# Attention: score steps of 128 and 256 columns run as one of 384, and the rotary step reads its product from PSUM

## The chip, the cores and the metric

The kernel runs on one core of a Trainium2 chip, as one program and one launch. The metric is the device time of that program in microseconds (us), as the median of several runs. Its engines are TensorE (PE; its weight loads are shown apart as PEld), VectorE (DVE), ScalarE (ACT), GpSimd (POOL) and the DMA queues, of which SP's issues most loads. Each engine takes its instructions in the order in which the program lists them; that order is made when the program is built.

## The reference

Two layers of width 1024 over 512 positions. Layer 0 is attention, layer 1 a gated delta rule; each is followed by a SwiGLU network. The change touches layer 0 alone, which has two kinds of heads, eight of each, 64 wide:

```python
def attention_head_groups(h, positions, w_in, w_out):
    proj = h @ w_in                                # q, k, v of both kinds
    qa, ka = partial_rope(qa, positions), partial_rope(ka, positions)
    oa = moba_attention(qa, ka, va)                # with 512 positions: causal softmax attention
    ob = stick_breaking_attention(qb, kb, vb)
    return concatenate([oa, ob]) @ w_out

# stick breaking, for the queries of one block, against all keys up to it
z = q @ k.T * scale
log_1m = where(causal, log_sigmoid(-z), 0.0)
log_after = cumsum(log_1m, reverse=True) - log_1m
w = where(causal, exp(log_sigmoid(z) + log_after), 0.0)
out = w @ v

# rope, on the first 16 of a head's 64 rows
[x1 * cos - x2 * sin, x2 * cos + x1 * sin, rest]
```

## The kernel before

All activations lie transposed, features on the 128 partitions and the 512 positions in the columns. Products are made in float32 from halves: a value is split into a rounded high part and the rest (`split`, line 246: ScalarE's copy writes the high part, VectorE's subtraction the low one, line 254), and each product is three matmuls of 512 columns (`gemm`, lines 337 to 340).

Layer 0 first makes q, k and v of the first pair of heads (lines 634 to 643). From then on it works in four pairs (line 809): for each of the two heads of a pair `moba` and `stick`, and then, as work to fill TensorE's waits, the four projections of the next pair (`proj`, line 703). `spread` (line 698) ties the 32 k-steps of these four projections to the 16 score products of the pair's two heads, so two k-steps may start after each of these (`gates`, `behind`). What runs when beyond that is set by the program's scheduler, by its own estimate of durations. Of the last pair, the first blocks of the output projection take that place (line 831). `proj` asks for weights two ahead; these come by DMAs that POOL issues (lines 291 and 293, the second adds in the DMA).

`finish` (line 648) takes a projection's product out of its PSUM bank (tag `mm`, three banks, line 199). For q and k of `moba` (rotary) ScalarE copies it to SBUF (line 651), VectorE swaps rows of the copy (653), POOL multiplies them by the sines (654) while VectorE multiplies the copy by the cosines (655), and VectorE adds the two (656). The result is split for each head.

`moba` (line 743) goes in four steps i, of 128, 256, 384 and 512 score columns: two matmuls and between them one of 128 columns that adds the causal mask in bfloat16 (lines 739 to 741) into the one bank `s`; the row maximum (753), the exponential with its sum (755), a reciprocal, the scaling, transposes into the one bank `pt` (768), and the split into `ph` and `pl`. Then `pv_out` multiplies by v (lines 730 to 732).

`stick` (line 773) goes in four steps j = 3, 2, 1, 0 of 128, 256, 384 and 512 columns, in two banks `z`: scores and mask as above, then on ScalarE absolute value, exponential and logarithm (789 to 791), VectorE's 792, a split into `ssh`, `ssl`, matmuls that add the sums over later keys to the bank (798), an exponential that frees it (800), and a split that POOL makes (804, 805; for the last head ScalarE and VectorE). It ends in `pv_out`. The tensors `sph`, `spl`, `ssh` and `ssl` hold the steps behind each other in the order 3, 2, 1, 0.

Between the heads VectorE also makes the conditioning vectors of both layers, one product of 1024 columns at a time (`ada`, line 210).

Of the kernel before, what the change touches and what calls it, by code (L numbers as in the profile page):

```python
# [71 lines left out]
ADA0 = 4  # L72
NACT = (1, 6)
# [462 lines left out]
def attention(e, x0ctx):  # L536
    nc, tc, V, G, A, PE, I = e.nc, e.tc, e.V, e.G, e.A, e.PE, e.I
    from contextlib import ExitStack
    with ExitStack() as ctx:
        p1 = ctx.enter_context(e.pool("at1"))  # L540

        C = p1.tile([128, T], F32, name="C")
# [49 lines left out]
        first = e.start()  # L592
# [19 lines left out]
        with e.psum_pool("start") as sp:  # L612
# [32 lines left out]
                    e.act_set()  # L645
            fin = ctx2.enter_context(e.pool("afin"))

            def finish(ps, name, scale, rope, dma):
                if rope:
                    q = fin.tile([128, T], F32, name="rq", bufs=2)  # L650
                    A.activation(q, ps, AF.Copy, scale=scale)
                    sw = fin.tile([128, T], F32, name="rs", bufs=1)
                    V.stream_shuffle(sw, q, swap)
                    G.tensor_tensor(sw, sw, S, op=OP.mult)
                    V.tensor_tensor(q, q, C, op=OP.mult)
                    V.tensor_tensor(q, q, sw, op=OP.add)
                    ps, scale = q, 1.0
                rows = [(slice(64 * head, 64 * head + 64), slice(64 - 64 * head, 128 - 64 * head)) for head in range(2)]
                if (name, 0) in twice:
                    assert scale == 1.0  # L660
                    for head, (rs, other) in enumerate(rows):
                        h, l = twice[name, head]
                        e.split(ps[rs], h[rs], l[rs])
                        if dma:
                            nc.sync.dma_start(h[other], h[rs])
                        else:
                            A.activation(h[other], ps[rs], AF.Copy)
                    return [twice[name, head] for head in range(2)]

                both = [qk.tile([128, T], F32R, name=f"{name}{head}", bufs=1) for head in range(2)]  # L670
                for t, (rs, other) in zip(both, rows):
                    A.activation(t[rs], ps[rs], AF.Copy, scale=scale)
                    V.scalar_tensor_tensor(t[other], ps[rs], scale, t[rs].bitcast(F32), op0=OP.mult, op1=OP.subtract)
                return both
# [10 lines left out]
            cur = [finish(pq[i], *KINDS[i], False) for i in range(4)]  # L685
# [10 lines left out]
        steps = []  # L696
# [6 lines left out]
        def proj(pair, i):  # L703
            w = e.load_w(("attn_in", (pair - 1) * 4 + i))
            ps = e.mm_tile()
            e.gemm(ps, w, hs, FULL)
            return finish(ps, *KINDS[i], False)

        def vproj(i):
            ws = [e.load_w(("attn_v", i, j)) for j in (0, 4)]  # L710
# [13 lines left out]
        def pv_out(chunk, r0, tag, ph, pl, at):  # L724

            o = psum.tile([128, T], F32, name="o", tag="o", bufs=1)
            vh, vl = vtile("ab"[chunk // 4], chunk % 4)
            for j in range(4):
                q = slice(j * 128, T)
                PE.matmul(o[:, q], vh[:, j], at(ph, j), start=j == 0, stop=False)  # L730
                PE.matmul(o[:, q], vl[:, j], at(ph, j), start=False, stop=False)
                PE.matmul(o[:, q], vh[:, j], at(pl, j), start=False, stop=j == 3)
            rs = slice(r0, r0 + 64)
            e.split(o[rs], ot[chunk][0][rs], ot[chunk][1][rs])

        def scores(ps, x, xs, y, ys, at, mask):

            xh, xl = x
            PE.matmul(ps, xh[:, xs], y[:, ys], start=True, stop=False)
            PE.matmul(ps[:, at], e.identb, mask, start=False, stop=False)  # L740
            steps[-1].append(PE.matmul(ps, xl[:, xs], y[:, ys], start=False, stop=True).ins)

        def moba(pair, h, q, k):

            ph = work.tile([128, 1664], F32R, name="ph", tag="ph", bufs=1)
            pl = work.tile([128, 1664], F32R, name="pl", tag="pl", bufs=1)
            for i in range(4):
                n = 128 * (i + 1)
                qs = slice(i * 128, n)
                s = psum.tile([128, T], F32, name="s", tag="s", bufs=1)  # L750
                scores(s[:, :n], q[h], qs, k[h], slice(0, n), qs, causal)
                st = work.tile([128, 3], F32, name="st", tag="st", bufs=4)
                V.tensor_reduce(st[:, 0:1], s[:, :n], AX.X, OP.max, negate=True)
                p = work.tile([128, T], F32, name="p", tag="p", bufs=2)
                A.activation(p[:, :n], s[:, :n], AF.Exp, bias=st[:, 0:1], accum_out=st[:, 1:2])
                ins = V.reciprocal(st[:, 2:3], st[:, 1:2])
                step = 4 * (2 * pair + h) + i - ADA0
                if 0 <= step < 24:
                    with tc.issue_after(ins.ins):
                        e.ada(0, 2 + step // 8, step % 8)  # L760
                if NACT[0] <= 2 * pair + h < NACT[1]:
                    A.activation(p[:, :n], p[:, :n], AF.Copy, scale=st[:, 2:3])
                else:
                    V.tensor_scalar(p[:, :n], p[:, :n], st[:, 2:3], None, op0=OP.mult)
                pt = psum.tile([128, T], F32, name="pt", tag="pt", bufs=1)
                for j in range(i + 1):
                    js = slice(j * 128, j * 128 + 128)
                    PE.transpose(pt[:, js], p[:, js], e.ident)
                src = pt[:, :n].rearrange("p (j q) -> p j q", q=128)
                e.split(src, *(x.rearrange("p (j q) -> p j q", q=128)[:, i:4 * i + 1:3] for x in (ph, pl)))  # L770
            pv_out(pair, h * 64, "m", ph, pl, lambda x, j: x[:, 512 * j:512 * j + 512 - 128 * j])

        def stick(pair, h, q, k):
            off = {3: 0, 2: 128, 1: 384, 0: 768}

            def at(x, j):
                return x[:, off[j]:off[j] + T - 128 * j]

            wh = work.tile([128, 1280], F32R, name="sph", tag="sph", bufs=1)
            wl = work.tile([128, 1280], F32R, name="spl", tag="spl", bufs=1)  # L780
            sh = work.tile([128, 1280], F32R, name="ssh", tag="ssh", bufs=1)
            sl = work.tile([128, 1280], F32R, name="ssl", tag="ssl", bufs=1)
            for j in (3, 2, 1, 0):
                n = T - 128 * j
                bank = ("pt", "s", "z", "z")[j] if (pair, h) == (3, 1) else "z"
                z = psum.tile([128, T], F32, name="z", tag=bank, bufs=2 if bank == "z" else 1)
                scores(z[:, :n], k[h], slice(j * 128, j * 128 + 128), q[h], slice(j * 128, T), slice(0, 128), strictT)
# [7 lines left out]
                for jj in range(3, j, -1):  # L795
                    mms = [(z[:, (jj - j) * 128:n], nones, at(x, jj)) for x in (sh, sl)] + mms
                for i, (o, m, x) in enumerate(mms):
                    PE.matmul(o, m, x, start=False, stop=i == len(mms) - 1, skip_group_check=True)
                w = e.wpool.tile([128, T], F32, name="sq", tag="sq", bufs=3)
                A.activation(w[:, :n], z[:, :n], AF.Exp)  # L800
                if (pair, h) >= LATE:
                    e.split(w[:, :n], at(wh, j), at(wl, j))
                else:
                    G.tensor_scalar(at(wh, j), w[:, :n], 1.0, 1.0, op0=OP.mult, op1=OP.mult)
                    G.tensor_tensor(at(wl, j), w[:, :n], at(wh, j).bitcast(F32), op=OP.subtract)
            pv_out(4 + pair, h * 64, "s", wh, wl, at)

        vproj(0)
        for p in range(4):
# [499 lines left out]
```

## Time and profile before

| what | us |
|---|---|
| median of 3 runs (1411.13 to 1413.59) | 1411.75 |
| the profiled execution, its own time | 1410.65 |
| its span, first to last instruction | 1408.8 |
| PE busy in the span | 1360.9 |
| DVE busy | 818.6 |
| ACT busy | 605.4 |
| POOL busy | 292.0 |

The stage that the change touches runs from about 66 us of the span, where the first projections end, to about 282, where the output projection has TensorE to itself. The views used below are the page's first part (busy time by engine), the table of windows (busy time by engine in each stretch, with the TensorE clock that was granted as a share of full speed), the waits (who waited for whom, how long, how often), the timeline (start, duration, what it is; in brackets the idle time before it and what ended that), and the groups of instructions by line and shape (busy time, mean duration in ns of one; then the idle time before them).

### The profile page before, as it was taken

To read this page: it belongs to the slowest core of one execution; us is meant where nothing else is said; L and a number is where in the kernel's file an instruction comes from. 1 tells how busy PE (TensorE), PEld (TensorE's weight loads), DVE (VectorE), ACT (ScalarE), POOL (GpSimd) and SP (SyncE) were. 2 spreads that over 40 slices of the span, in tenths; PEclk is the share of its full clock that TensorE was granted. 3 is DMA by queue.
4 is the path that set the end of the run, shared out by engine and by line. 5 is a ranking of instruction groups with operands and counts; after the bars stand their busy time and mean duration, and the time that the engine had idled before them with its cause. 6 is when DMAs were issued, how large, how long until landed. Compare 5 with 4: busy or idle time off the path is not lost.

```text
span 1408.8 us, 19224 instructions
## 1 busy us (share of the span) xinstructions
PE 1360.9 (97%) x7354; PEld 1158.4 (82%) x7354; DVE 818.6 (58%) x1422; ACT 605.4 (43%) x1162; POOL 292.0 (21%) x279
## 2 busy tenths in 40 slices
PE   7999999899999999999999899999999999999997
PEld 4787787698888888889888787888998888888887
DVE  6777879655667667323878796446783333333233
ACT  5577888744222222223557533356662222222221
POOL 4024444110111111000024735311001111110010
PEclk9999999999999999999999999999999999999999
DMA  9537674042667666434522314312452333333332
GB/s 367 164 75 193 171 181 159 30 166 65 219 217 241 233 236 221 131 106 152 177 62 75 105 60 120 106 46 90 151 180 73 93 94 101 96 99 94 97 102 68
DMA packets 58734, 190.66 MB, mean 135 GB/s; under 512 B 7081, under 2 KB 11305, under 8 KB 58642
## 3 DMA queue, kind: packets, MB, share of 16 engines
q1 hardware_dynamic: 53376, 173.56, 38.0%
q0 software_dynamic: 4112, 14.82, 4.8%
q8 instruction: 58, 0.95, 0.3%
q10 hardware_dynamic: 1154, 1.05, 0.2%
q14 instruction: 34, 0.28, 0.1%
HBM read 184.11 MB, written 5.29 MB: 134 GB/s over the span
## 4 chain that ended last, share of the span: by engine, by line
PE 84%; DVE 6%; ACT 4%; DMA 3%; POOL 1%; issue 1%; SPq 0%; DVEq 0%; ACTq 0%; POOLq 0%
PE mm L337 21%; PE mm L338 21%; PE mm L340 21%; DMA wh<-in_attn_in_dram 1%; PE f L340 1%; PE f L338 1%; PE f L337 1%; PE mm L1117 1%; PE mm L1115 1%; PE mm L1116 1%; PE bank L949 1%; DVE DT L1009 1%; DMA call<-in_consts_dram 1%; PE bank L1051 1%; PE mm L719 1%
## 5 line engine op out<-in xcount | busy, mean ns | idle before, releaser
L249 ACT ACTIVATE wh<-raw 128x1024 fp32r<-128x1024 f32 (+1 forms) x203 | 211.5, 1042 | 535.5 <-PE mm L338 488.9
L254 DVE TENSOR_TENSOR wl<-raw,wh 128x1024 fp32r<-128x1024 f32 (+1 forms) x193 | 231.9, 1202 | 192.1 <-ACT wh L249 176.0
L337 PE MATMUL mm<-hh,wh 128*128 128x512 f32 (+1 forms) x776 | 290.0, 377 | 0.7 <-ACT wh L249 0.6
L338 PE MATMUL mm<-hl,wh 128*128 128x512 f32 (+1 forms) x776 | 288.0, 374 | 0.0
L340 PE MATMUL mm<-hh,wl 128*128 128x512 f32 (+1 forms) x776 | 243.2, 374 | 0.0
L337 PEld LDWEIGHTS mm<-hh,wh 128*128 128x128 f32 x776 | 146.6, 189 | 25.2 <-ACT wh L249 1.1
L338 PEld LDWEIGHTS mm<-hl,wh 128*128 128x128 f32 x776 | 146.9, 189 | 24.2
L340 PEld LDWEIGHTS mm<-hh,wl 128*128 128x128 f32 x776 | 142.7, 189 | 25.2
L214 DVE CUSTOM_DVE_ANT_0 aw<-aw,cond 128x1024 f32<-128x1024 f32 x96 | 126.2, 1333 | 5.9 <-DMA aw<-in_ada_w_dram 5.8
L251 POOL TENSOR_SCALAR ah<-ac 128x512 fp32r<-128x512 f32 x36 | 53.3, 1482 | 363.9 <-DVE ac L497 363.9
L338 PE MATMUL mm<-h1l,wh 128*128 128x512 f32 x320 | 124.5, 389 | 0.0
L337 PE MATMUL mm<-h1h,wh 128*128 128x512 f32 x320 | 124.5, 389 | 0.0
L338 PE MATMUL mm<-al,wh 128*128 128x512 f32 (+1 forms) x354 | 124.0, 355 | 0.0
L337 PE MATMUL mm<-ah,wh 128*128 128x512 f32 (+1 forms) x354 | 123.7, 355 | 0.2 <-ACT ah L249 0.2
L497 DVE TENSOR_TENSOR ac<-sg,mm 128x512 f32<-128x512 f32 x40 | 27.5, 688 | 146.5 <-PE mm L340 143.1
L340 PE MATMUL mm<-h1h,wl 128*128 128x512 f32 x320 | 105.0, 389 | 0.0
L340 PE MATMUL mm<-ah,wl 128*128 128x512 f32 (+1 forms) x354 | 103.8, 355 | 0.0
L337 PEld LDWEIGHTS mm<-ah,wh 128*128 128x128 f32 x354 | 66.5, 188 | 9.9 <-ACT ah L249 0.5
L338 PEld LDWEIGHTS mm<-al,wh 128*128 128x128 f32 x354 | 66.6, 188 | 9.4
L340 PEld LDWEIGHTS mm<-ah,wl 128*128 128x128 f32 x354 | 63.9, 188 | 9.4
L338 PEld LDWEIGHTS mm<-h1l,wh 128*128 128x128 f32 x320 | 60.1, 188 | 12.5
L337 PEld LDWEIGHTS mm<-h1h,wh 128*128 128x128 f32 x320 | 60.0, 188 | 12.5
(395 smaller groups left out, 2484.5 us busy)
## 6 DMA issues: line engine op xcount, KB each, us to landing
aw<-in_ada_w_dram SPq DMA_DIRECT2D x96, 512.0 KB
raw<-in_ffn_in_dram SPq DMA_DIRECT2D x88, 512.0 KB
raw<-in_ffn_out_dram SPq DMA_DIRECT2D x36, 512.0 KB
raw<-in_gdn_in_dram SPq DMA_DIRECT2D x26, 512.0 KB
raw<-in_gdn_z_dram SPq DMA_DIRECT2D x16, 512.0 KB
raw<-in_gdn_out_dram SPq DMA_DIRECT2D x16, 512.0 KB
raw<-in_ffn_out_dram SPq DMA_DIRECT2D x18, 384.0 KB
wh<-in_attn_in_dram POOLq DMA_DIRECT2D x12, 512.0 KB, 4.8
```

The costliest lines, as they stand in the source:

```text
L214: return V.tensor_tensor_reduce(w, w, cond, 1.0, 0.0, OP.mult, OP.add, mod[:, j:j + 1])
L249: ins = A.activation(h, src, AF.Copy)
L251: G.tensor_scalar(h, src, 1.0, 1.0, op0=OP.mult, op1=OP.mult)
L254: (G if eng == "p" else V).tensor_tensor(l, src, h.bitcast(F32), op=OP.subtract)
L337: PE.matmul(ps, wh[k][:, 0], xh[:, cs], start=first and i == 0, stop=False)
L338: PE.matmul(ps, wh[k][:, 0], xl[:, cs], start=False, stop=False)
L340: PE.matmul(ps, wl[j][:, 0], x[j][0][:, cs], start=False, stop=last and j == order[-1])
L497: ins = V.tensor_tensor(ac, sg, pu, op=OP.mult)
L719: PE.matmul(ps, xh[:, t], wl, start=False, stop=False)
L949: PE.matmul(ps[:, c], lhs[:, cs], rhs[:, cs], start=True, stop=True)
L1009: V.tensor_tensor(d, DS[:, :m, m:m + 1].to_broadcast([128, m, w]), DV[:, m:m + 1, m:].to_broadcast([128, m, w]), op=OP.mult)
L1051: PE.matmul(p4[:, c], U[h][lo, c], x[lo, c, lo], start=True, stop=True)
```

## The change

In `finish`, ScalarE's copy is gone. VectorE's row swap and its multiplication by the cosines read the product in PSUM. The factor 0.125 of q, which that copy applied, is applied by the copies and the subtraction that split q; both copies of a head now stand ahead of the subtraction.

In `moba`, steps 1 and 0 share the bank `s` (256 and 128 columns, behind each other). Their maxima, exponentials, reciprocals and scalings stay apart, but the transposes go into one bank `pt` and one split of 384 columns takes them out. In `stick`, steps 3 and 2 share one bank `z`; absolute value, exponentials, logarithm, VectorE's operation and both splits run once over 384 columns, and so do the matmuls with `ntri`. Steps 2 and 3 of `moba` and 1 and 0 of `stick` stay alone.

The mask comes ahead of the scores, as the matmul that starts the bank; for a merged step one matmul of 256 columns writes it for both. `ph` and `pl` are packed to 1280 columns, in an order in which each group's columns lie together, so that `pv_out` reads blocks of 128 columns at a distance of two or four blocks.

```diff
-            def finish(ps, name, scale, rope, dma):
+            def finish(ps, name, scale, rope):
                 if rope:
                     q = fin.tile([128, T], F32, name="rq", bufs=2)
-                    A.activation(q, ps, AF.Copy, scale=scale)
                     sw = fin.tile([128, T], F32, name="rs", bufs=1)
-                    V.stream_shuffle(sw, q, swap)
+                    V.stream_shuffle(sw, ps, swap)
                     G.tensor_tensor(sw, sw, S, op=OP.mult)
-                    V.tensor_tensor(q, q, C, op=OP.mult)
+                    V.tensor_tensor(q, ps, C, op=OP.mult)
                     V.tensor_tensor(q, q, sw, op=OP.add)
-                    ps, scale = q, 1.0
+                    ps = q
...
-                        e.split(ps[rs], h[rs], l[rs])
-                        if dma:
-                            nc.sync.dma_start(h[other], h[rs])
-                        else:
-                            A.activation(h[other], ps[rs], AF.Copy)
+                        for to in (rs, other):
+                            A.activation(h[to], ps[rs], AF.Copy, scale=scale)
+                        V.scalar_tensor_tensor(l[rs], ps[rs], scale, h[rs].bitcast(F32), op0=OP.mult, op1=OP.subtract)
...
+        def masked(ps, first, n, mask):
+            PE.matmul(blocks(ps, first, 1, n), e.identb, mask[:, None, :].to_broadcast([128, n, 128]),
+                      start=True, stop=False, skip_group_check=True)
...
-            PE.matmul(ps, xh[:, xs], y[:, ys], start=True, stop=False)
-            PE.matmul(ps[:, at], e.identb, mask, start=False, stop=False)
-            steps[-1].append(PE.matmul(ps, xl[:, xs], y[:, ys], start=False, stop=True).ins)
+            PE.matmul(ps, xh[:, xs], y[:, ys], start=False, stop=False, skip_group_check=True)
+            steps[-1].append(PE.matmul(ps, xl[:, xs], y[:, ys], start=False, stop=True, skip_group_check=True).ins)
...
+            place = {0: (0,), 1: (2, 1), 2: (4, 5, 3), 3: (6, 9, 7, 8)}
+            rows = ((0, 2, 4), (1, 4, 3), (3, 4, 2), (8, 1, 1))
-            for i in range(4):
+            for group in ((1, 0), (2,), (3,)):
...
+                masked(s, group[0], len(group), causal)
+                at = {1: 0, 0: 256, 2: 0, 3: 0}
+                for i in group:
+                    scores(s[:, at[i]:at[i] + 128 * (i + 1)], q[h], slice(i * 128, i * 128 + 128), k[h],
+                           slice(0, 128 * (i + 1)))
...
+                e.split(pt[:, :128 * n], *(x[:, base * 128:(base + n) * 128] for x in (ph, pl)))
...
-            for j in (3, 2, 1, 0):
+            for group in ((3, 2), (1,), (0,)):
...
+                masked(z, 0, len(group), strictT)
+                for j in group:
+                    scores(z[:, off[j] - base:off[j] - base + T - 128 * j], k[h], slice(j * 128, j * 128 + 128),
+                           q[h], slice(j * 128, T))
...
-                e.split(u[:, :n], at(sh, j), at(sl, j))
-                mms = [(z[:, :n], ntri, at(x, j)) for x in (sh, sl)]
+                e.split(u[:, :n], sh[:, here], sl[:, here])
+                mms = [(z[:, :n], ntri, x[:, here]) for x in (sh, sl)]
```

## Rows read from the trace of the kernel before

**Rows 1.** The page's first part: busy us of each engine, its share, its instructions.

```profile
PE 1360.9 (97%) x7354; PEld 1158.4 (82%) x7354; DVE 818.6 (58%) x1422; ACT 605.4 (43%) x1162; POOL 292.0 (21%) x279
```

**Rows 2.** Windows, start to columns: stretch, its us, busy us by engine, clock, DMA.

```profile
66.00:84.00 18.00, 14.87 (x105) 14.24 (x104) 16.20 (x38) 13.73 (x37) 3.21 (x3) 0.91 0.18 59
84.00:242.00 158.00, 151.29 (x865) 126.61 (x863) 124.00 (x251) 126.14 (x296) 64.44 (x73) 0.99 0.63 167
242.00:282.00 40.00, 34.71 (x195) 27.34 (x195) 25.62 (x58) 29.37 (x73) 9.75 (x12) 1.00 0.13 41
```

**Rows 3.** Waits of PE from 66 to 282: us in total, times, longest.

```profile
PE mm L719 <- DVE wl L254: 3.1, 1, 3.1
PE z L739 <- ACT sq L800: 3.0, 4, 1.8
...
PE s L739 <- ACT p L755: 1.3, 2, 0.8
```

**Rows 4.** Timeline at the stage's start: start us, us, engine, line, what.

```profile
66.12 0.60 ACT L651 ACTIVATE rq<-pq 128x512 f32<-128x512 f32 x1 [1.88 <-PE pq L636]
...
66.76 0.75 DVE L653 STREAM_SHUFFLE rs<-rq 128x512 f32<-128x512 f32 x1
...
67.59 1.30 POOL L654 TENSOR_TENSOR rs<-rs,S 128x512 f32<-128x512 f32 x1 [29.76 <-DVE rs L653]
67.60 1.83 DVE L655 TENSOR_TENSOR rq<-rq,C 128x512 f32<-128x512 f32 x1
...
71.98 1.21 DVE L254 TENSOR_TENSOR wl<-raw,wh 128x1024 fp32r<-128x1024 f32 x1
...
73.24 0.39 PE L719 MATMUL mm<-wl,hh 128*128 128x256 f32 x1 [3.13 <-DVE wl L254]
...
75.48 0.41 PE L718 MATMUL mm<-wh,hh 128*128 128x256 f32 x1
```

**Rows 5.** ACT by line and shape, 66 to 282: busy us, mean ns, idle.

```profile
L651 ACT ACTIVATE rq<-mm 128x512 f32<-128x512 f32 x7 | 4.1, 589 | 0.6 <-PE mm L340 0.6
...
L789 ACT ACTIVATE u<-z 128x384 f32<-128x384 f32 x8 | 3.9, 486 | 0.7 <-PE z L741 0.6
...
L789 ACT ACTIVATE u<-z 128x256 f32<-128x256 f32 x8 | 3.0, 380 | 0.2
...
L789 ACT ACTIVATE u<-z 128x128 f32<-128x128 f32 x8 | 2.2, 272 | 1.4 <-PE z L741 1.4
```

**Rows 6.** The same for DVE.

```profile
L655 DVE TENSOR_TENSOR rq<-rq,C 128x512 f32<-128x512 f32 x8 | 10.1, 1266 | 0.2
...
L656 DVE TENSOR_TENSOR rq<-rq,rs 128x512 f32<-128x512 f32 x8 | 5.5, 690 | 1.3 <-POOL rs L654 1.2
...
L792 DVE SCALAR_TENSOR_TENSOR u<-z,u 128x512 f32<-128x512 f32 x8 | 5.5, 688 | 0.7 <-ACT u L791 0.6
...
L792 DVE SCALAR_TENSOR_TENSOR u<-z,u 128x384 f32<-128x384 f32 x8 | 4.4, 548 | 2.8 <-ACT u L791 2.8
...
L792 DVE SCALAR_TENSOR_TENSOR u<-z,u 128x256 f32<-128x256 f32 x8 | 3.3, 417 | 0.7 <-ACT u L791 0.7
L792 DVE SCALAR_TENSOR_TENSOR u<-z,u 128x128 f32<-128x128 f32 x8 | 2.3, 285 | 2.0 <-ACT u L791 2.0
```

**Rows 7.** The same for POOL.

```profile
L804 POOL TENSOR_SCALAR sph<-sq 128x384 fp32r<-128x384 f32 x7 | 8.0, 1136 | 22.4 <-ACT sq L800 22.4
...
L804 POOL TENSOR_SCALAR sph<-sq 128x512 fp32r<-128x512 f32 x7 | 5.7, 820 | 10.8 <-ACT sq L800 10.8
```

**Rows 8.** Timeline of PE around one score step of 512 columns.

```profile
155.46 0.39 PE L739 MATMUL z<-qb,kbh 128*128 128x512 f32 x1
155.69 0.23 PE L740 MATMUL z<-strictT,identb 128*128 128x128 bf16 x1
155.72 0.48 PE L741 MATMUL z<-qb,kbl 128*128 128x512 f32 x1
156.04 0.39 PE L338 MATMUL mm<-hl,wh 128*128 128x512 f32 x1
```

More of the change, by code (lines that the diff above doesn't have):

```diff
@@ L684, in attention @@
             V.tensor_scalar(nones, e.ones, -1.0, None, op0=OP.mult)
-            cur = [finish(pq[i], *KINDS[i], False) for i in range(4)]
+            cur = [finish(pq[i], *KINDS[i]) for i in range(4)]
             for c in range(4):
@@ L706, in proj @@
             e.gemm(ps, w, hs, FULL)
-            return finish(ps, *KINDS[i], False)
+            return finish(ps, *KINDS[i])
         def vproj(i):
@@ L728, in pv_out @@
             for j in range(4):
[L729 to L732, printed above, removed]
+                q = o[:, j * 128:].rearrange("p (b q) -> p b q", q=128)
+                PE.matmul(q, vh[:, j], at(ph, j), start=j == 0, stop=False)
+                PE.matmul(q, vl[:, j], at(ph, j), start=False, stop=False)
@@ L733, in pv_out, with blocks @@
+                PE.matmul(q, vh[:, j], at(pl, j), start=False, stop=j == 3)
             rs = slice(r0, r0 + 64)
             e.split(o[rs], ot[chunk][0][rs], ot[chunk][1][rs])
-        def scores(ps, x, xs, y, ys, at, mask):
+        def blocks(x, first=0, step=1, n=None):
+            b = x.rearrange("p (b q) -> p b q", q=128)
+            return b[:, first:None if n is None else first + (n - 1) * step + 1:step]
+        def masked(ps, first, n, mask):
+            PE.matmul(blocks(ps, first, 1, n), e.identb, mask[:, None, :].to_broadcast([128, n, 128]),
+                      start=True, stop=False, skip_group_check=True)
@@ L738, in scores @@
+        def scores(ps, x, xs, y, ys):
             xh, xl = x
-            PE.matmul(ps, xh[:, xs], y[:, ys], start=True, stop=False)
-            PE.matmul(ps[:, at], e.identb, mask, start=False, stop=False)
-            steps[-1].append(PE.matmul(ps, xl[:, xs], y[:, ys], start=False, stop=True).ins)
+            PE.matmul(ps, xh[:, xs], y[:, ys], start=False, stop=False, skip_group_check=True)
+            steps[-1].append(PE.matmul(ps, xl[:, xs], y[:, ys], start=False, stop=True, skip_group_check=True).ins)
@@ L743, in moba @@
         def moba(pair, h, q, k):
-            ph = work.tile([128, 1664], F32R, name="ph", tag="ph", bufs=1)
-            pl = work.tile([128, 1664], F32R, name="pl", tag="pl", bufs=1)
-            for i in range(4):
-                n = 128 * (i + 1)
-                qs = slice(i * 128, n)
+            place = {0: (0,), 1: (2, 1), 2: (4, 5, 3), 3: (6, 9, 7, 8)}
+            rows = ((0, 2, 4), (1, 4, 3), (3, 4, 2), (8, 1, 1))
+            ph = work.tile([128, 1280], F32R, name="ph", tag="ph", bufs=1)
@@ L750, in moba @@
+            pl = work.tile([128, 1280], F32R, name="pl", tag="pl", bufs=1)
+            for group in ((1, 0), (2,), (3,)):
                 s = psum.tile([128, T], F32, name="s", tag="s", bufs=1)
-                scores(s[:, :n], q[h], qs, k[h], slice(0, n), qs, causal)
-                st = work.tile([128, 3], F32, name="st", tag="st", bufs=4)
-                V.tensor_reduce(st[:, 0:1], s[:, :n], AX.X, OP.max, negate=True)
                 p = work.tile([128, T], F32, name="p", tag="p", bufs=2)
-                A.activation(p[:, :n], s[:, :n], AF.Exp, bias=st[:, 0:1], accum_out=st[:, 1:2])
@@ L756, in moba @@
[L756 to L764, printed above, removed]
@@ L765, in moba @@
-                pt = psum.tile([128, T], F32, name="pt", tag="pt", bufs=1)
[L766 to L771, printed above, removed]
+                masked(s, group[0], len(group), causal)
@@ new lines, in moba @@
+                at = {1: 0, 0: 256, 2: 0, 3: 0}
+                for i in group:
+                    scores(s[:, at[i]:at[i] + 128 * (i + 1)], q[h], slice(i * 128, i * 128 + 128), k[h],
+                           slice(0, 128 * (i + 1)))
+                for i in group:
+                    c = slice(at[i], at[i] + 128 * (i + 1))
+                    st = work.tile([128, 3], F32, name="st", tag="st", bufs=4)
+                    V.tensor_reduce(st[:, 0:1], s[:, c], AX.X, OP.max, negate=True)
+                    A.activation(p[:, c], s[:, c], AF.Exp, bias=st[:, 0:1], accum_out=st[:, 1:2])
+                    ins = V.reciprocal(st[:, 2:3], st[:, 1:2])
+                    step = 4 * (2 * pair + h) + i - ADA0
+                    if 0 <= step < 24:
+                        with tc.issue_after(ins.ins):
+                            e.ada(0, 2 + step // 8, step % 8)
+                    if NACT[0] <= 2 * pair + h < NACT[1]:
+                        A.activation(p[:, c], p[:, c], AF.Copy, scale=st[:, 2:3])
+                    else:
+                        V.tensor_scalar(p[:, c], p[:, c], st[:, 2:3], None, op0=OP.mult)
@@ new lines, in moba @@
+                pt = psum.tile([128, T], F32, name="pt", tag="pt", bufs=1)
+                base = min(b for i in group for b in place[i])
+                n = sum(i + 1 for i in group)
+                for i in group:
+                    for j, b in enumerate(place[i]):
+                        PE.transpose(pt[:, (b - base) * 128:(b - base + 1) * 128],
+                                     p[:, at[i] + j * 128:at[i] + j * 128 + 128], e.ident)
+                e.split(pt[:, :128 * n], *(x[:, base * 128:(base + n) * 128] for x in (ph, pl)))
@@ L773, in stick @@
+            pv_out(pair, h * 64, "m", ph, pl, lambda x, j: blocks(x, *rows[j]))
         def stick(pair, h, q, k):
@@ L782, in stick @@
             sl = work.tile([128, 1280], F32R, name="ssl", tag="ssl", bufs=1)
-            for j in (3, 2, 1, 0):
-                n = T - 128 * j
-                bank = ("pt", "s", "z", "z")[j] if (pair, h) == (3, 1) else "z"
+            for group in ((3, 2), (1,), (0,)):
+                bank = {1: "s", 0: "pt"}.get(group[0], "z") if (pair, h) == (3, 1) else "z"
                 z = psum.tile([128, T], F32, name="z", tag=bank, bufs=2 if bank == "z" else 1)
-                scores(z[:, :n], k[h], slice(j * 128, j * 128 + 128), q[h], slice(j * 128, T), slice(0, 128), strictT)
+                base = off[group[0]]
+                n = sum(T - 128 * j for j in group)
+                here = slice(base, base + n)
+                masked(z, 0, len(group), strictT)
+                for j in group:
+                    scores(z[:, off[j] - base:off[j] - base + T - 128 * j], k[h], slice(j * 128, j * 128 + 128),
+                           q[h], slice(j * 128, T))
                 u = work.tile([128, T], F32, name="u", tag="u", bufs=2)
@@ L792, in stick @@
                 V.scalar_tensor_tensor(u[:, :n], z[:, :n], 0.0, u[:, :n], op0=OP.max, op1=OP.add)
-                e.split(u[:, :n], at(sh, j), at(sl, j))
-                mms = [(z[:, :n], ntri, at(x, j)) for x in (sh, sl)]
-                for jj in range(3, j, -1):
-                    mms = [(z[:, (jj - j) * 128:n], nones, at(x, jj)) for x in (sh, sl)] + mms
+                e.split(u[:, :n], sh[:, here], sl[:, here])
+                mms = [(z[:, :n], ntri, x[:, here]) for x in (sh, sl)]
+                for j in group:
+                    for jj in range(3, j, -1):
+                        c = off[j] - base + (jj - j) * 128
+                        mms = [(z[:, c:off[j] - base + T - 128 * j], nones, at(x, jj)) for x in (sh, sl)] + mms
+                if len(group) > 1:
+                    mms = mms[2:] + mms[:2]
                 for i, (o, m, x) in enumerate(mms):
@@ L801, in stick @@
                 if (pair, h) >= LATE:
-                    e.split(w[:, :n], at(wh, j), at(wl, j))
+                    e.split(w[:, :n], wh[:, here], wl[:, here])
                 else:
-                    G.tensor_scalar(at(wh, j), w[:, :n], 1.0, 1.0, op0=OP.mult, op1=OP.mult)
-                    G.tensor_tensor(at(wl, j), w[:, :n], at(wh, j).bitcast(F32), op=OP.subtract)
-            pv_out(4 + pair, h * 64, "s", wh, wl, at)
+                    G.tensor_scalar(wh[:, here], w[:, :n], 1.0, 1.0, op0=OP.mult, op1=OP.mult)
+                    G.tensor_tensor(wl[:, here], w[:, :n], wh[:, here].bitcast(F32), op=OP.subtract)
+            pv_out(4 + pair, h * 64, "s", wh, wl, lambda x, j: blocks(at(x, j)))
         vproj(0)
```

1 line of the change is left out of this document (removed).

## The prediction

> **What bounds the kernel now.** I read the page's first part first: TensorE is busy for 1360.9 us of the span, 97%, so a gain has to come out of the few places where TensorE waits, runs at the lower clock or has less to do [rows 1]. The table of windows then gives the stage that the change touches, 66 to 282 us, in three parts: its start, the middle with the four pairs' heads and projections mixed, and the last pair, whose only other work is the first blocks of the output projection. TensorE is idle there for 18 - 14.87 = 3.1, 158 - 151.29 = 6.7 and 40 - 34.71 = 5.3 us, 15.1 in all [rows 2]. Behind 282 us nothing is changed and TensorE's work is the same, so I carry the stage's end over to the kernel's end one to one. The reader should see that ScalarE (13.73 + 126.14 + 29.37 = 169.2 us) and VectorE (165.8) are each busy for three quarters of the stage: neither is the bound, but TensorE waits for both.
>
> The waits of TensorE say for what: once 3.1 us for VectorE's low halves of the weights of v at the start, four times, 3.0 us, for the exponential that frees a bank `z`, twice, 1.3 us, for the exponential that frees `s` [rows 3]; the rest is spread over nine more reasons. [...]
>
> **The rotary step.** Removed are eight copies of 0.59 us, 4.7 us of ScalarE [rows 5]. VectorE's swap starts when the product is there, not behind the copy: 66.12 for 66.76 at the start [rows 4]. The multiplication by the cosines takes 1266 ns in the mean, the addition two instructions later, of the same shape and also out of SBUF, 690 [rows 6]. The timeline shows why: it began at 67.60, within 0.01 us of POOL's multiplication by the sines, and took 1.83 us [rows 4]. With its first operand in PSUM I take 0.69: the operation of line 792, with one operand in PSUM, takes 688 [rows 6]. That is 8 x 0.58 = 4.6 us of VectorE. The bounds are nothing, if it still collides with POOL, and 1.14 at the start. What a swap out of PSUM costs no row shows; line 792 against line 656 (688 to 690) says the same as out of SBUF, and I take that; 0.3 us more or less for each would be 2.4 us of VectorE, off the path but for the first one.
>
> [...]
>
> VectorE now holds the bank `mm` until the cosines are in. The bank is wanted again three projections later, and each is 24 matmuls of 0.23 us, 5.5 us at least [rows 8]; that hides it, and with VectorE over 10 us behind it would be TensorE's wait. The split's copies and subtractions are as many as before; putting both copies ahead of the subtraction I count at nothing, since the matmuls wait for the last of the three anyway.
>
> **The merged steps.** In `stick` absolute value, two exponentials, logarithm and the split's copy, in `moba` the split's copy run once over 384 columns instead of over 128 and 256. For line 789 that is 272 + 380 - 486 = 166 ns [rows 5]; six such in eight heads are 8.0 us of ScalarE. For line 792 it is 285 + 417 - 548 = 154 ns [rows 6]; three such (the operation and two subtractions) in eight heads are 3.7 us of VectorE. So ScalarE loses 12.7 of 169.2 us and VectorE 8.3 of 165.8. For POOL's split I count nothing: 384 columns took 1136 ns where 512 took 820 [rows 7], so its durations follow who else runs, not the columns; over seven heads that leaves a bound of 2 us either way, on an engine with 77 of 216 us busy [rows 2].
>
> TensorE loses one mask matmul in each of 16 merged steps. A score step of 512 columns went from 155.46 to 156.04, 0.58 us for two matmuls of 0.23: the mask costs 0.12 [rows 8]. The remaining mask has 128 columns more, 0.06. So 16 x 0.06 = 1.0 us; the ends are 0 and 1.9. The columns with `ntri` stay the same; the saving of their issue is inside that bound. Packing `ph` and `pl` I count at nothing: the same columns, in blocks of 128; no row shows a moving operand with such a step, and if it cost TensorE 10% of the 96 matmuls (0.06 to 0.23 us each, some 14 us) it would be 1.4 us. The order of the conditioning's loads moves by one place within a head, on SP's queue, which only prefetches.
>
> **The sum,** against the profiled execution (1410.65 us, of which 1408.8 are its span). At the start VectorE's queue gets 0.64 us (no copy ahead) and 1.83 - 0.69 = 1.14 us ahead: the wait of 3.1 us shrinks by 1.8. What is late next is POOL's fetch of the pair's weights, which isn't needed before TensorE is through with v. With 1.3 us of idle time left I take it that the clock stays up: 1.6. Fewer masks: 1.0. In the middle and at the end each of `moba` and `stick` makes three round trips to ScalarE and VectorE in place of four, so I take a quarter of the idle time off: 1.7 and 1.3. Against it, the first results of a merged step come later: three operations of 486 for 272 and one of 548 for 285 are 0.9 us a head. In the first three pairs projections fill that; without them it would be 5.4 us more. In the last pair I count it, 1.8. Together 1.8 + 1.6 + 1.0 + 1.7 + 1.3 - 1.8 = 5.6: 1405.05. The profiled execution lay 1.1 us under the median, so 1406.2 as a median.
>
> **The rivals.**
> Coarser filling (slower). The score products of a merged step stand next to each other, so the four k-steps tied to them (12 matmuls, 2.8 us) are let go at once, and the second half of what used to be two rounds has none of its own (1.4 us before). If TensorE eats the lump early, the end of the round stands open. For it: the idle time already sits in such places [rows 3]. Against it: the work of the other head kind is also there, and 6.7 us idle in 158 say that filling is ample [rows 2]. There are twelve such rounds in the pairs with projections; from 5.6 / 12 = 0.47 us each the gain is gone, at 0.9 it is 10.8 - 5.6 = 5.2 slower: 1417. 16%.
> The wait is replaced (no change). TensorE's idle time in the middle and at the end stays, because the next thing late (POOL's splits, POOL's weight loads behind them) ends where the old one did; left are the start without the clock and the masks less the later results, 1.8 + 1.0 - 1.8 = 1.0: 1410.8, with 1409 to 1414 around it. 17%.
> The collision with POOL stays, PSUM or not. The start gains 0.64 only and keeps the low clock: 5.6 - 1.14 - 1.6 = 2.9, so 1408.9, half of it on either side of the bound below. 12%.
> More than a quarter. If ScalarE's 12.7 us take half of the idle time in the middle and at the end, the terms there are 3.4 and 2.6 and the coarser step costs nothing: 5.6 + 3.0 + 1.8 = 10.4: 1401.3. 12%.
>
> **How the numbers follow.** The forecast, 1403 to 1408.9, has 43%. A measurement of this kernel tells about 0.2%, 2.8 us, from no change. Faster by more than that (under 1408.9): 43 + 12 + 6 = 61%; within it: 6 + 17 = 23%; slower: 16%. The range of 8 in 10 leaves out half of the largest gain and the greater part of the slower case: 1400 to 1415.
>
> **What would show it.** Right: line 651 gone and the eight multiplications by the cosines near 0.69; TensorE's first wait 1.3 us and no matmul at the lower clock near 75 us; ScalarE some 12 us less busy in the stage; 48 mask matmuls for 64; the stage's end 5 to 6 us earlier and the rest of the span as it was. Wrong: longer waits of TensorE for 755, 800 or the splits of the merged steps; k-steps of the projections bunched behind merged scores with idle time after them; a swap out of PSUM well over 0.74 us; waits for a bank `mm`.

## The result, and the profile after

The changed kernel takes 1404.24 us (median of 6 runs, 1401.29 to 1406.22) where the kernel before, run beside it, takes 1411.44: a ratio of 0.9947 with a 95% interval of 0.9935 to 0.9959, so 5.8 to 9.2 us faster. The forecast was 1406.2 with 1400 to 1415. Its profiled execution took 1405.91, one of the longer ones, with a span of 1404.1. Size and sign came as forecast; the terms of the sum did not, as the following sections show.

Where the time went is seen in three views of the changed kernel. First the page's busy times and the table of windows (stretch, its us, busy us by engine, granted clock, DMA), which answer to [rows 1, 2]:

```profile
PE 1359.1 (97%) x7322; PEld 1159.4 (83%) x7322; DVE 819.9 (58%) x1397; ACT 596.0 (42%) x1105; POOL 282.8 (20%) x265
```

```profile
66.00:84.00 18.00, 15.54 (x102) 14.51 (x101) 16.73 (x40) 12.84 (x35) 3.22 (x3) 0.91 0.20 59
84.00:242.00 158.00, 153.42 (x891) 131.25 (x890) 129.77 (x247) 125.37 (x268) 60.35 (x65) 1.00 0.65 170
242.00:282.00 40.00, 35.23 (x169) 28.03 (x168) 23.81 (x42) 25.27 (x49) 6.42 (x7) 0.87 0.32 100
```

TensorE is idle for 2.5, 4.6 and 4.8 us where it was 3.1, 6.7 and 5.3. The first stretch still has the clock of 0.91. The last one now has 0.87: the clock is 0.50 in each us from 268 to 277, 0.74 in the one ahead and 0.64 in the one behind, where the kernel before has 1.00 throughout. ScalarE has 9.4 us less in all; VectorE has 1.3 us more, not 8.3 less.

The first residual addition marks the end of the stage. In the view of line 411 (duration min/median/max in ns, first and last start) of before and of after:

```profile
L411 DVE SCALAR_TENSOR_TENSOR x<-mm,fin,x x22: 479/484/751, 282.2 to 682.4; 128x256 f32<-128x256 f32 x12, 128x512 f32<-128x512 f32 x10
```

```profile
L411 DVE SCALAR_TENSOR_TENSOR x<-mm,fin,x x22: 477/486/752, 277.5 to 677.3; 128x256 f32<-128x256 f32 x12, 128x512 f32<-128x512 f32 x10
```

From there to the end of the span are 1126.6 us in both (1408.8 - 282.2, 1404.1 - 277.5). The difference of 4.7 us lies wholly ahead of it, and the stage itself gained more: the first rotary product was there at 67.5 us and not at 66.1 [rows 4], in a part that the change doesn't touch (TensorE's first 194 matmuls are the same and in the same order; from 40 to 50 us this execution was granted 0.72 of the clock, the one before 0.83). So the stage took 210.0 us where it took 216.1.

The waits of TensorE from 60 to 282 us (us in total, times, longest), to set beside [rows 3]:

```profile
PE mm L714 <- DVE qb L669: 2.5, 1, 2.5
PE o L726 <- ACT ph L249: 1.8, 2, 1.5
PE z L822 <- DVE u L812: 1.6, 2, 1.3
PE o L726 <- ACT sph L249: 1.3, 1, 1.3
PE s L739 <- ACT p L767: 1.2, 1, 1.2
...
PE z L739 <- ACT sq L824: 0.5, 1, 0.5
```

The wait for the exponential that frees a bank `z` fell from 3.0 to 0.5 us. The wait at the start has only changed its cause: it was for the weights of v, it is now for VectorE's work on `qb`. The timeline of after shows it (start, us, what):

```profile
67.54 0.73 DVE L652 STREAM_SHUFFLE rs<-pq 128x512 f32<-128x512 f32 x1
...
68.17 0.67 DVE L654 TENSOR_TENSOR rq<-pq,C 128x512 f32<-128x512 f32 x1
...
71.61 0.69 DVE L669 SCALAR_TENSOR_TENSOR qb<-mm,qb 64x512 fp32r<-64x512 f32 x1
...
72.34 0.75 DVE L652 STREAM_SHUFFLE rs<-mm 128x512 f32<-128x512 f32 x1
72.45 0.36 PE L714 MATMUL mm<-wh,hh 128*128 128x256 f32 x1 [2.46 <-DVE qb L669]
...
73.12 0.69 DVE L654 TENSOR_TENSOR rq<-mm,C 128x512 f32<-128x512 f32 x1
...
75.39 0.41 PE L716 MATMUL mm<-wh,hl 128*128 128x256 f32 x1
```

The three banks `mm` hold ka, qb and kb when the first projections end, and v's projection wants one. Before, ScalarE's copy of ka gave one back at once, and v's first matmul ran at 68.42:

```profile
66.61 0.59 ACT L651 ACTIVATE rq<-mm 128x512 f32<-128x512 f32 x1
...
68.42 0.28 PE L718 MATMUL mm<-wh,hh 128*128 128x256 f32 x1
```

Now ka's bank is held until VectorE's swap and cosines at 72.34 and 73.12; qb's comes free first, behind the subtraction that ends at 72.30, and TensorE starts at 72.45. The matmul of 0.41 us at 75.39 shows the lower clock again: 0.50 is granted from 74 to 76 us, and at 77, with 1.00, matmuls of this shape take 0.28.

### The profile page after: what moved, and what is told of

Same layout as the page of the kernel before. It is cut to its first block, busy times and chain, and to the rows that moved or that the text cites. A ratio compares the mean times of both kernels' runs of the same rounds, so it can differ in the third digit from the quotient of the medians.

```text
span 1404.1 us, 19043 instructions
## 1 busy us (share of the span) xinstructions
PE 1359.1 (97%) x7322; PEld 1159.4 (83%) x7322; DVE 819.9 (58%) x1397; ACT 596.0 (42%) x1105; POOL 282.8 (20%) x265
## 4 chain that ended last, share of the span: by engine, by line
PE 84%; DVE 6%; DMA 4%; ACT 3%; issue 1%; POOL 1%; SPq 0%; DVEq 0%; ACTq 0%; POOLq 0%
PE mm L337 21%; PE mm L338 21%; PE mm L340 21%; DMA wh<-in_attn_in_dram 1%; PE f L340 1%; PE f L338 1%; PE f L337 1%; PE mm L1141 1%; PE mm L1139 1%; PE mm L1140 1%; PE bank L973 1%; DVE DT L1033 1%; DVE aw L214 1%; DMA call<-in_consts_dram 1%; DMA wl<-in_attn_in_dram 1%
## 5 line engine op out<-in xcount | busy, mean ns | idle before, releaser
L340 PEld LDWEIGHTS mm<-h1h,wl 128*128 128x128 f32 x320 | 60.1, 188 | 12.4
```

What stands on the lines that cost most here:

```text
L340: PE.matmul(ps, wl[j][:, 0], x[j][0][:, cs], start=False, stop=last and j == order[-1])
```

## Experiments

All times are against the kernel before, run on the same chip between them; the experiments ran in three groups on three chips, so rows are compared by their ratios. All of these kernels make the whole computation. The table gives each ratio with its 95% interval, and in us what it is of 1412.

| kernel | ratio | us |
|---|---|---|
| the change | 0.9947 (0.9935 to 0.9959) | -7.5 |
| rotary part alone | 1.0038 (1.0023 to 1.0052) | +5.4 |
| both merges alone | 1.0002 (0.9990 to 1.0014) | +0.3 |
| `stick` merged alone | 1.0132 (1.0115 to 1.0148) | +18.6 |
| `moba` merged alone | 1.0047 (1.0034 to 1.0060) | +6.6 |
| rotary part, TensorE in before's order | 0.9994 (0.9984 to 1.0005) | -0.8 |
| merges, TensorE in the changed kernel's order | 0.9993 (0.9984 to 1.0002) | -1.0 |
| the change, TensorE in the merges' order | 0.9984 (0.9973 to 0.9995) | -2.3 |
| before, TensorE in the rotary part's order | 1.0085 (1.0072 to 1.0098) | +12.0 |
| merges, all engines in the changed kernel's order | 1.0051 (1.0036 to 1.0066) | +7.2 |
| rotary part, all engines in before's order | 1.0049 (1.0037 to 1.0061) | +6.9 |
| the change, first ka copied by ScalarE, TensorE's order held | 0.9940 (0.9927 to 0.9954) | -8.5 |
| the change, k-steps spread over merged steps | 0.9935 (0.9921 to 0.9948) | -9.2 |

**The parts alone.** The first question was which part carries the gain. The rotary part is the diff's `finish` put into the kernel before; the merges are the rest of the diff with the old `finish`; the other two put only `stick`'s or only `moba`'s new function there.

> The new rotary step and split alone, steps unmerged and the mask between the score products as before. By the forecast's sum it carries the start: 1.8 for the shorter wait and 1.6 for the clock, so 3.4 us faster than before. By the theory read from the changed kernel's trace (at the start the bank of ka is now held until VectorE's swap and cosines, TensorE's wait only went from 3.1 to 2.5 us and the clock fell all the same) the start gives under 1 us; what else it gives comes from 4.7 us less of ScalarE in the middle: 0 to 2 us faster in all.

> Both merges, mask first and packing, with the old rotary step. By the forecast's sum 1.0 + 1.7 + 1.3 - 1.8 = 2.2 us faster than before. By the theory that the merges carry the gain: 5 to 7 us faster. If the two parts add up, this and the rotary step alone sum to the change's 7.2 us; if they don't, the order of instructions, which is made anew for each program, moves the time by the difference.

> Only stick is merged (and has its mask first); moba and the rotary step are as before. By the forecast's count it holds five of the six operations that ScalarE loses by merging and two of VectorE's three, so if the gain follows the work taken off these engines, some five sixths of what both merges give. If it follows the round trips saved, one in each kind of head, half of it.

> Only moba is merged (mask first, packed halves); stick and the rotary step are as before. If the gain follows the work taken off ScalarE and VectorE, one sixth of what both merges give, within 0.2% of before; if it follows the round trips saved, half of it, 2 to 3 us. If the packed halves' blocks cost TensorE, the matmuls with v take longer than 0.06 to 0.23 us apart and it is slower.

All four missed. No part alone is faster: +5.4 for the rotary part, +0.3 for the merges, and one merge alone is worse than both together, +18.6 and +6.6. The parts do not add up: +5.4 and +0.3 stand against -7.5. The packed halves are not what makes the last one slow: its matmuls with v in `moba` start 0.11, 0.12, 0.18 and 0.23 us apart (medians by shape), as in the kernel before. The waits of TensorE show what is late in each (same view as above; the merges, then `stick` alone):

```profile
PE mm L340 <- DMA wl<-in_attn_in_dram: 8.6, 3, 4.9
PE mm L719 <- DVE wl L254: 3.1, 1, 3.1
```

```profile
PE mm L340 <- DMA wl<-in_attn_in_dram: 5.1, 1, 5.1
PE z L743 <- ACT sq L838: 3.3, 3, 1.8
```

With the merges alone TensorE stands 8.6 us for the adding DMA of a projection's weights, 0.5 us in the changed kernel, none before. Its list puts the low halves of a projection ahead of the moment at which they land, and TensorE runs nothing else in that time. With `stick` alone the clock is lower too, 0.84 from 140 to 180 us and 0.85 from 260 to 306, where the kernel before has 0.96 and 1.00. So the order of instructions is a suspect: it is made anew from the scheduler's estimates for each program, and a part of the change gives another one.

**The order of TensorE held.** To part the order from the work, TensorE's matmuls are tied into a list taken from another program that holds the same ones (6938 in the kernels with the old steps, 6906 in those with the merged ones; all but 47 are tied). An edge adds no wait for another engine; it says only what is issued first. In the traces TensorE's order is then that of the other program from the first matmul to the last:

```diff
+    mms = [i for i in nc.cur_bb.bb.instructions if type(i).__name__ == MM]
...
+    info = mybir.DependencyInfo(mybir.DependencyClass.NoSync, mybir.DependencyReason.DATA)
+    for a, b in zip(order, order[1:]):
+        tc.add_manual_dep(mms[b], mms[a].name, info, reason="pin")
```

> The rotary part alone, as in e1, but TensorE's instructions are held in the order that they have in the kernel before (both hold the same 6938 matmuls); the other engines' order is still made by the scheduler. If e1's 5 us of loss come from the new order of TensorE's instructions, it falls to before or under it: 0 to 3 us faster, which is then what the rotary part's work is worth. If the work itself costs (banks held longer, the first projection of v late by 2.5 us), it stays 4 to 6 us slower.

> Both merges with the old rotary step, as in e2, but TensorE's 6906 matmuls in the order that they have in the changed kernel. If the order decides, it comes near the changed kernel: 5 to 8 us faster than before. If the rotary part's 4.7 us of ScalarE are what the changed kernel gains over e2, it stays near before, 0 to 2 us faster.

> The changed kernel in full, with TensorE's matmuls in the order of e2, the merges alone. If the order decides, the 7 us are gone and it stands near e2, within 2 us of before. If the work taken off ScalarE and VectorE decides, it stays 5 to 7 us faster.

> The kernel before, unchanged in its work, with TensorE's matmuls in the order of e1, the rotary part alone. If the order decides, it is 4 to 6 us slower than before with no work added. If e1's loss is the rotary part's work, it stays within 2 us of before.

First compare pairs with the same order of TensorE, without and with the rotary part's work. The pair with the work is faster in each of four orders: in before's order 0 to -0.8 (inside the interval of none), in the rotary part's own +12.0 to +5.4, so 6.6; in the merges' +0.3 to -2.3, 2.6; in the changed kernel's -1.0 to -7.5, 6.5. Then compare pairs with the same work and another order of TensorE. The difference is as large: the rotary part's own order costs 12.0 us with the work of before and 6.2 with its own (+5.4 for -0.8); the merges' order costs 1.3 and 5.2 against that of the changed kernel. In all these pairs the other engines' order is still made by the scheduler and differs too, so no difference is the price of the work, or of TensorE's order, alone.

The expectation that "the order decides" had the sign right for the kernel before in another order, but not the size: it lost 12.0 us with its work unchanged, where 4 to 6 were expected. It fell for the merges: in the changed kernel's order they gained 1.3 us of 7.8. In the kernel before with the other order the waits are spread over the whole stage, and the clock is 0.81 in its first 18 us and 0.87 in its last 40, where it was 0.91 and 1.00 [rows 2]:

```profile
PE mm L722 <- DVE qb L677: 4.2, 1, 4.2
PE z L743 <- ACT sq L804: 3.9, 4, 1.5
PE z L802 <- DVE u L796: 3.6, 3, 2.0
PE z L743 <- ACT kbh L671: 2.7, 1, 2.7
```

**The order of all engines held.** In those runs the other engines' order was still free. Here such edges tie VectorE, ScalarE, POOL and SP as well.

> The merges with the old rotary step, and on every engine (TensorE, VectorE, ScalarE, POOL, SP) the order of the changed kernel; only the eight copies of the rotary step are placed by the scheduler. It differs from the changed kernel by the rotary part's work alone. If that work is worth what f2 against the changed kernel says (TensorE's order held: 6.3 us), it is within 2 us of before. If the other engines' order made that difference, it stands near the changed kernel, 5 to 7 us faster than before.

> The rotary part alone, and on every engine the order of the kernel before. It differs from before by the rotary part's work alone. By f1 (TensorE's order held) 0.8 us faster; by the forecast's sum 3.4 us for the start. If the same work is worth 6 us in the merged order and 1 here, its worth depends on what the order leaves late.

Both came out slower than with TensorE alone held: the merges +7.2 for -1.0, the rotary part +6.9 for -0.8. So neither theory's number held, and the other engines' order alone moved the time by some 8 us, with the work and TensorE's order the same. Where every engine's order is the same, the rotary part's work is worth 14.7 us in the changed kernel's order (+7.2 to -7.5) and costs 6.9 in before's. What holding an order costs by itself is not known: no run holds a kernel to its own order on every engine. (With TensorE's order alone held to the changed kernel's own, the run that frees the bank, below, is at -8.5.)

The rotary part in before's full order is the plain case, the work off ScalarE and VectorE and nothing moved, and it loses 6.9 us. Its waits say where:

```profile
PE mm L724 <- DVE qb L679: 6.6, 1, 6.6
PE z L745 <- ACT sq L806: 3.7, 4, 1.6
PE s L745 <- ACT p L761: 2.9, 5, 1.0
PE mm L724 <- DVE kbl L673: 1.8, 1, 1.8
```

6.6 and 1.8 us at the start are for the banks `mm`, which VectorE now empties in the old order; before, the start waited 3.1 us in all. The clock of the first 18 us is 0.74 for 0.91. Matched matmul by matmul with the kernel before, it is 0.1 us early at 68 us of its span, 6.7 late at 85 and 8.0 to 8.5 from 254 on, so most of the loss is this start. The merges with the changed kernel's full order, matched with the changed kernel, lose in many places: they are 1.7 us early at 66 us of their span, 3.0 late at 87, 5.9 at 163, 9.5 at 199 and 14.0 at 253. The added copies run at 66, 66, 126, 134, 161, 166, 209 and 217; the largest later step, from 6.5 to 9.5 between 173 and 199, follows no copy closely, so what each step is due to is not shown.

**The bank at the start.**

```diff
-            def finish(ps, name, scale, rope):
+            def finish(ps, name, scale, rope, copy=False):
...
+                    if copy:
+                        A.activation(q, ps, AF.Copy)
+                        ps = q
...
-            cur = [finish(pq[i], *KINDS[i]) for i in range(4)]
+            cur = [finish(pq[i], *KINDS[i], i == 1) for i in range(4)]
```

> The changed kernel, TensorE's matmuls in its order, but the first pair's ka is copied to SBUF by ScalarE, as before the change, which gives its bank back for the projection of v. If the bank is what TensorE waits 2.5 us for at the start of the stage, that wait goes and the kernel is 1 to 3 us faster than the changed one (8 to 10 faster than before); v's projection then waits for the low halves of its weights. If the wait moves there in full, no change to the changed kernel.

The bank was the cause of that one wait: v's projection starts at once, at 68.20 behind the last matmul ahead of it, and the first stretch is at the full clock, as the windows show:

```profile
66.00:84.00 18.00, 14.92 (x110) 13.62 (x109) 15.98 (x39) 14.21 (x38) 3.21 (x3) 1.00 0.19 59
```

But no gain is shown in the end: 0.9940 with an interval that reaches over the change's 0.9947. The same line says why: TensorE is idle there for 18 - 14.92 = 3.1 us, more than the 2.5 of the changed kernel. In place of the one wait stand four, one for the weights of v and three for banks `mm` that VectorE's work on `kbl`, `bl` and `qb` frees:

```profile
PE mm L721 <- DVE kbl L670: 1.0, 1, 1.0
PE mm L721 <- ACT wh L253: 0.9, 1, 0.9
PE mm L721 <- DVE bl L258: 0.8, 1, 0.8
PE mm L721 <- DVE qb L676: 0.4, 1, 0.4
```

Matched matmul by matmul with the changed kernel, it is 1.6 us early at 66 us of the changed kernel's span, ahead of anything that the edit touches, 4.3 at v's first matmul, and 1.8 at 83. So of the 2.6 us that the bank gave, 0.2 are left 10 us later. At 166 it is 2.6 us early and at 173 level, and by 175 1.2 us late. There stand 3.4 us at the lower clock (0.99 granted from 84 to 242 us, 1.00 in the changed kernel) and a wait that the changed kernel had not:

```profile
PE mm L344 <- DMA wl<-in_attn_in_dram: 2.0, 1, 2.0
```

One of the adding DMAs of this stretch (140 to 185 us) took 9.2 us from issue to landing, where the longest in the changed kernel took 7.1. The start's gain was gone before that. The time can't tell the two outcomes of the expectation apart (-8.5 fits its 8 to 10 as well); the trace speaks for the second, the wait moves.

**Coarser filling.**

```diff
-            steps[-1].append(PE.matmul(ps, xl[:, xs], y[:, ys], start=False, stop=True, skip_group_check=True).ins)
+            ins = PE.matmul(ps, xl[:, xs], y[:, ys], start=False, stop=True, skip_group_check=True).ins
+            if gate:
+                steps[-1].append(ins)
```

`gate` is false for the second score product of a merged step; in its place the step's last transpose (`moba`) or last sum (`stick`) is entered.

> The changed kernel with the k-steps of the next pair's projections spread over a merged step: the second pair of them is tied to the group's last transpose (moba) or last sum (stick), not to the second score product. By the rival of coarser filling it gains 3 to 6 us over the changed kernel. By the theory that the order made anew decides, it lands anywhere within some 6 us of it, and the sign says nothing on the filling unless TensorE's idle time behind merged scores falls.

The ratio of 0.9935 is 1.7 us below the change's and its interval overlaps the change's: no gain is shown, and the rival's 3 to 6 us are not shown either, though the intervals leave room for 3. It is the fastest median of all (1403.81, against 1412.82 for before beside it), but no better version than the change as far as these runs tell. Its profile has TensorE's idle time at 2.5, 4.4 and 3.7 us, as in the changed kernel but for the end, and no lower clock there:

```profile
242.00:282.00 40.00, 36.26 (x190) 29.13 (x189) 23.51 (x38) 25.03 (x46) 6.49 (x7) 1.00 0.34 106
```

## Why the prediction was right, and where it was not

**The start (1.8 + 1.6) failed.** The step was "that hides it": the bank `mm` that VectorE holds would be wanted three projections later. At the start all three banks are full at once and v's projection comes directly behind them; behind that, no long wait for a bank `mm` stands in the list of the changed kernel. The wait shrank from 3.1 to 2.5 us, and the clock stayed at 0.91. No run shows the 1.6 us that the sum has for the clock: the one run with 1.00 over these 18 us, with the first ka copied, is at 0.9940 where the change is at 0.9947, inside each other's intervals. What is late next was also wrong: the prediction names POOL's fetch of weights. The run that frees the bank shows the weights of v and VectorE's work on `kbl`, `bl` and `qb` instead: of the 2.6 us that the freed bank gives, 0.2 are left 10 us later.

**VectorE's operation out of PSUM was right in itself.** The multiplication takes 677 ns in place of 1266, the swap 743 in place of 740. All eight multiplications overlapped POOL's arithmetic, by 0.3 to 0.6 us, and took 665 to 692 ns; in the kernel before, out of SBUF, seven overlapped it: five took 1.44 to 1.83 us, and in the two that took 0.69 POOL's multiplication took 1.78 and 1.80. Yet the sum of 8.3 us less for VectorE was wrong. In the groups by line and shape (busy us, mean ns, idle before) of after, then of before:

```profile
L663 DVE SCALAR_TENSOR_TENSOR qal<-rq,qah 64x512 fp32r<-64x512 f32 x8 | 8.8, 1098 | 0.2
L655 DVE TENSOR_TENSOR rq<-rq,rs 128x512 f32<-128x512 f32 x8 | 6.5, 810 | 0.3 <-POOL rs L653 0.2
...
L652 DVE STREAM_SHUFFLE rs<-mm 128x512 f32<-128x512 f32 x7 | 5.2, 743 | 0.0
L654 DVE TENSOR_TENSOR rq<-mm,C 128x512 f32<-128x512 f32 x7 | 4.7, 677 | 0.0
```

```profile
L254 DVE TENSOR_TENSOR qal<-rq,qah 64x512 fp32r<-64x512 f32 x8 | 6.5, 818 | 1.3 <-ACT qah L249 1.1
```

The collision has moved: instructions with both operands in SBUF that used to run beside an idle POOL now run beside a busy one, the subtraction for q 1098 ns for 818, the addition of the rotary step 810 for 690 [rows 6]. One by one: five of the eight subtractions for q overlap POOL's arithmetic by 0.8 us or more and take 883 to 1517 ns, the other three 685 to 690; in the kernel before one did (1749 ns), and the others took 671 to 690. The merges met the same: three of the sixteen subtractions of `ssl` over 384 columns take 1169 to 1533 ns beside POOL's split, so that this one operation gave 0.2 us of the 1.2 counted for it. A fixed pair of instructions was freed of the collision; the time on POOL was still there to collide with.

**Fewer masks and merged operations were right in number.** 48 mask matmuls stand for 64 and 32 matmuls in all are gone (7354 to 7322). ScalarE has 9.4 us less on the page, where 12.7 were counted: its instructions overlap in part, and added up one by one over the stage they are 13.3 us less (195.9 to 182.6). What the 1.0 us for the masks came to was not measured by itself.

**The middle and the end (1.0 + 1.7 + 1.3 - 1.8 = 2.2) were too small.** The stage gained 6.1 us in the profiled executions, of which the first window's idle time is 0.6; the idle time in the middle fell by 2.1 and the wait for banks `z` by 2.5. The step that failed here is the form of the sum. It priced each part's work as if the order of instructions stayed, and added. The runs show that it doesn't stay and that nothing adds: the same rotary work gains 0.8 to 6.6 us with TensorE's order held, and with every engine's order held it loses 6.9 in before's order and gains 14.7 in the changed kernel's; the same work of before is 12.0 us slower in another order; and the two parts that are +5.4 and +0.3 alone are -7.5 together. That 5.6 was near 7.2 is luck: one term was too large by 3, the others too small by 4.

**The rivals.** Coarser filling is not shown: spreading it gained nothing outside the intervals. The collision with POOL stays: not at that instruction, but elsewhere, as above. The wait is replaced: at the start this is what happened, though for the kernel as a whole its 1410.8 us did not come. In the three kernels with a merge and the old rotary step TensorE waits 8.6, 5.1 and 3.8 us for the weights' DMA, which the kernel before never did in this stage.

**What stays open.** Why the change as a whole gains 7.2 us is shown only so far: most of it lies in the stage, outside the first wait, and in these runs it came only with all of the work in the order made with it. What the merges are worth by themselves in a given order can't be read from these runs, because their matmuls are not those of the kernel before and its order can't be imposed on them. And whether the order that came with the whole change is a lucky one among many, or the merges leave the scheduler's estimate nearer to the chip, was not settled; the one other order tried with the change's full work lost 5.2 of its 7.5 us.

## What to carry to other kernels

Where a scheduler orders the instructions from its own estimates, an edit has two effects, its work and a new order. Here they could not be priced apart: the order moved the time by up to 12 us with the work unchanged, and the same work was worth anything from 6.9 us lost to 14.7 gained by the order it ran in. Holding the order of the busiest engine alone was not enough to part them; hold every engine's, and time a kernel held to its own order beside it. A part that loses alone can be the part that gains in company, so a change of several parts is judged as a whole. And before a copy that empties a PSUM bank is taken out, look at every place where all banks are full at once: what counts is the work between two uses of a bank at the busiest point, not at the usual one. And look behind a wait before taking it out: here four smaller ones stood behind it.

## What the runs showed of the hardware

A multiplication on VectorE with one operand in PSUM took 665 to 692 ns all eight times, seven of them beside POOL's multiplication of 1.28 to 1.33 us; the same one out of SBUF took 1.44 to 1.83 us five times of the seven that it ran beside POOL's arithmetic, and 0.69 the other two, where POOL's multiplication took 1.78 and 1.80.

The clock did not follow the sum of TensorE's idle time: the stage's first 18 us had 0.91 behind one unbroken wait, of 3.1 us in the kernel before and of 2.5 in the changed one, and 1.00 where as much idle time (3.1 us) came in four waits of at most 1.0, with the first ka copied. In the last 40 us the profiled execution of the change had 0.87 with 4.8 us idle, and the kernel before 1.00 with 5.3; what tells these two apart is not shown.
